# A two-layer encoder trunk on one core: pair sums by accumulating DMAs, the embedding operand split earlier, other first and last stage, and TensorE operands at other offsets modulo 256 bytes

## The chip, the cores and the metric

The kernel runs on one core of a Trainium2 chip. TensorE (PE) multiplies, its weight loads appear as PEld, VectorE (DVE), ScalarE (ACT) and GpSimd (POOL) work element by element, and DMA queues of SyncE (SP), ACT and POOL move data between HBM and SBUF. The metric is device time in microseconds (us) of one launch; less is better. One profiled execution gives the trace from which all views come.

## The reference

Two layers, one sequence of 512 tokens, width 1024, everything in 32-bit floats. Each layer does this (x holds the tokens, `g` are gains):

```python
h = rmsnorm(x, norm1_g[i])
z = h @ w_in[i] + b_in[i]                      # 12296 columns: mLSTM, retention and gates
hm = mlstm_chunkwise(...)                      # 4 heads, causal conv + silu on q and k
hr = retention_chunkwise(...)                  # 4 heads, rotary on q and k
merged = sigmoid(gm) * (y_m @ w_bm[i]) + sigmoid(gr) * (y_r @ w_br[i])
x = x + merged @ w_out[i]
h2 = rmsnorm(x, norm2_g[i])
x = x + square(relu(h2 @ w_ff1[i] + b_ff1[i])) @ w_ff2[i] + b_ff2[i]   # 4096 hidden columns
h3 = rmsnorm(x, norm3_g[i])
x = x + sigmoid(h3 @ w_pe_gate[i]) * (p[i] @ w_pe[i])                  # p: 512 x 256, the embedding
```

After the second layer `rmsnorm(x, final_g)` is the output. `rmsnorm(x, g)` is `x * rsqrt(mean(x*x) + 1e-6) * g`.

## The kernel before

**Layout.** x lies transposed in SBUF: eight tiles (`KT`) of 128 columns of the width by 512 tokens (`T`). Each fp32 operand is split in two: a high part that TensorE's fp32r type holds (a copy by ACT), and the rest, the low part (a subtraction by DVE). A product is then three matmuls, high by high, high by low, low by high (`mm3`, L295 to L298). `split` (L230 to L232) makes both parts.

**Weights.** All weights come in one stream of units of 128 x 1024 floats (512 KB), in the order of use (`wstream`, on SP's queue). `fill_raws` keeps up to four raw units (`wr`) under way; `prep_next` (L253) splits the next one into pieces `wh` and `wl`; `unit` and `ready` do so two units ahead of the matmuls that use them. A unit of kind T8 gives one tile of 128 output columns: eight steps of `mm3` with 512 moving columns, 24 matmuls, into one PSUM bank.

**Norms.** `Norm` multiplies by the gain and splits (`operand`, L388), squares (`square`, L393), adds the squares of seven tiles with POOL into `sum` (L409) and keeps the eighth as `tail`. `finish` (L411) sends sum and tail through TensorE against `ones` to get one column of token sums, and POOL takes the power -1/2 (L422). `spread` (L424) makes a row of factors from it by a diagonal matrix and TensorE (`rb`). The factor is applied to the result of a product, not to its operand, so that matmuls start before the norm is known. In the last group of ff2 each x tile that is complete goes through `Norm.tile` for norm 3 (`l0n3`, `l1n3`).

**ff1 and ff2.** `ff_order` sets the sequence: the hidden layer is made in four blocks b of four parts p. `ff1(b, p)` is two T8 units; the result is squared, cut in quarters of 256 tokens and columns, and combined to 7 operands of 256 columns (`pair_quarters`, `pair_operand`). `ff2(b, p)` is a pair of weight units with a seven-product scheme in the manner of Strassen (P1 to P7, 12 matmuls of 256 columns each, 84 in a pair). Its weight pieces are B11 (512 columns) and the sums t1, t2, t3: `prep_next` computes the sums from the two raw units r1 and r2 with four DVE additions of 128 x 512 (L269, L270, L273, L277; c0 and c1 are the two halves), then splits them. Products of P4 run one pair late (`pair_schedule`). `done` (L952) adds each product to x on DVE (L950). The tile t is a single buffer, as each of the pieces of the pair.

**Embedding.** After the last ff1 the embedding operand `pth`, `ptl` is loaded and split (L987 to L991), and two units give p @ w_pe (48 matmuls, `l0pe`, `l1pe`). Then the last group of four pairs runs, and then the gate product (`pg`).

**First stage.** Two weight units are sent for, then x in four transfers of 512 KB. The eight operands of norm 1 follow, then the other raw units, then the squares, five of them on POOL. The first unit is the small one for the input and forget gates (`l0if`); the first wide one is `l0m0z`.

**Last stage.** The last four gate units of layer 1 are kept (`LAST`), and each is run over the first 256 tokens and then over the last 256 (tiles `pl`), with one final norm for each half (`l1n40`, `l1n41`). `final` (L1047) multiplies the x tiles by the factors, three on POOL and five on DVE, and four transfers write each half.

A scheduler places the instructions in each engine's queue by the order of the program and the buffers, so that the order in a queue is not that of the text. Every engine takes its own queue in order. `shift` (L205) puts a small unused tile at the start and the end of some pools, by which the addresses of the tiles after it move.

## Time and profile before

| what | before |
|---|---|
| median of 3 runs | 2441.95 us (2439.2 to 2444.41) |
| the profiled execution | 2438.42 us |
| its span, first to last instruction | 2436.7 us |
| mean granted TensorE clock | 0.993 |
| PE busy | 2390.5 us (98%) |
| DVE, ACT, POOL busy | 1574.1, 1042.2, 142.1 us |
| moved by DMA | 241.41 MB, mean 99 GB/s |

A row of a group reads: line of the kernel, engine, operation, output<-inputs, count, shortest, median and longest duration in ns, first and last start in us, shape. A matmul's duration includes its way through the array; the time from one start to the next is shorter. A row of waits says which line of which engine waited, on whom, for how long in all, how often, and the longest. The clock is the share of full speed that the throttle granted to TensorE.

### The profile page before, as it was taken

The numbers are of one execution on the slowest core, as the hardware profiler recorded it, in microseconds if no ns is written. First come the engines' busy times: TensorE is split into PE (matmuls) and PEld (weight loads), VectorE is DVE, ScalarE is ACT, GpSimd is POOL, SyncE is SP. The second block draws the span as 40 slices with busy tenths as digits, with TensorE's granted clock in tenths as the row PEclk, the third lists the DMA queues.
The fourth block names the chain that finished last, engine by engine and source line by source line (L and its number), as shares of the span: only waits on it lengthen the run. The fifth ranks groups of instructions, "written<-read, shape, count | busy, mean of one in ns | idle before, by whom it ended". The sixth has DMA issues, their size and how long they took to land.

```text
span 2436.7 us, 30731 instructions
## 1 busy us (share of the span) xinstructions
PE 2390.5 (98%) x12220; PEld 2040.2 (84%) x12220; DVE 1574.1 (65%) x2403; ACT 1042.2 (43%) x1420; POOL 142.1 (6%) x213
## 2 busy tenths in 40 slices
PE   8999999999999999998999999999999999999997
PEld 6888888888888899898888888888888888998786
DVE  7867536663555678777778665466635547788675
ACT  4746323332333545544446552233333335445443
POOL 4100000000001000000201000000000010000012
PEclk9999999999999999999999999999999999999998
DMA  4222232223234332332322222222232342332221
GB/s 165 93 89 77 83 104 87 86 85 132 78 121 130 113 104 87 104 113 72 132 90 89 91 83 95 95 95 82 92 120 87 122 134 90 113 104 96 95 87 44
DMA packets 74417, 241.41 MB, mean 99 GB/s; under 512 B 8089, under 2 KB 10521, under 8 KB 74273
## 3 DMA queue, kind: packets, MB, share of 16 engines
q1 hardware_dynamic: 64336, 221.49, 27.3%
q10 hardware_dynamic: 9936, 17.96, 2.4%
q8 instruction: 96, 1.57, 0.3%
q14 instruction: 49, 0.39, 0.0%
HBM read 231.02 MB, written 8.39 MB: 98 GB/s over the span
## 4 chain that ended last, share of the span: by engine, by line
PE 95%; DVE 3%; ACT 1%; issue 1%; POOL 0%; DVEq 0%; ACTq 0%; POOLq 0%
PE l0f L296 2%; PE l1f L296 2%; PE l1f L297 2%; PE l0f L297 2%; PE l0f L298 2%; PE l1f L298 2%; PE l1br L297 1%; PE l1br L296 1%; PE l0br L298 1%; PE l0br L297 1%; PE l0br L296 1%; PE l1br L298 1%; PE l1bgm L296 1%; PE l0bgm L296 1%; PE l0wo L297 1%
## 5 line engine op out<-in xcount | busy, mean ns | idle before, releaser
L231 ACT ACTIVATE wh<-wr 128x1024 fp32r<-128x1024 f32 x342 | 361.7, 1059 | 851.8 <-issue 161.4
L232 DVE TENSOR_TENSOR wl<-wr,wh 128x1024 fp32r<-128x1024 f32 x342 | 419.1, 1227 | 216.0 <-ACT wh L231 215.7
L231 ACT ACTIVATE wh_t<-wr 128x1024 fp32r<-128x1024 f32 x64 | 66.9, 1058 | 84.6 <-DVE wr L270 53.6
L296 PE MATMUL l0f<-l0n2h,wh 128*128 128x512 f32 x256 | 99.8, 390 | 0.0
L296 PE MATMUL l1f<-l1n2h,wh 128*128 128x512 f32 x256 | 99.8, 390 | 0.0
L298 PE MATMUL l1f<-l1n2h,wl 128*128 128x512 f32 x256 | 99.7, 389 | 0.0
L298 PE MATMUL l0f<-l0n2h,wl 128*128 128x512 f32 x256 | 99.7, 389 | 0.0
L297 PE MATMUL l1f<-l1n2l,wh 128*128 128x512 f32 x256 | 99.7, 389 | 0.0
L297 PE MATMUL l0f<-l0n2l,wh 128*128 128x512 f32 x256 | 99.6, 389 | 0.0
L232 DVE TENSOR_TENSOR wl_t<-wr,wh_t 128x1024 fp32r<-128x1024 f32 x64 | 77.1, 1218 | 19.4 <-ACT wh_t L231 19.2
L231 ACT ACTIVATE wh_t<-t 128x1024 fp32r<-128x1024 f32 x32 | 33.9, 1061 | 58.6 <-DVE t L277 14.2
L298 PEld LDWEIGHTS l0f<-l0n2h,wl 128*128 128x128 f32 x256 | 48.1, 188 | 10.2
L298 PEld LDWEIGHTS l1f<-l1n2h,wl 128*128 128x128 f32 x256 | 48.1, 188 | 10.1
L297 PEld LDWEIGHTS l0f<-l0n2l,wh 128*128 128x128 f32 x256 | 48.1, 188 | 9.8
L297 PEld LDWEIGHTS l1f<-l1n2l,wh 128*128 128x128 f32 x256 | 48.1, 188 | 9.7
L296 PEld LDWEIGHTS l1f<-l1n2h,wh 128*128 128x128 f32 x256 | 48.1, 188 | 9.7
L296 PEld LDWEIGHTS l0f<-l0n2h,wh 128*128 128x128 f32 x256 | 48.1, 188 | 9.6
L232 DVE TENSOR_TENSOR wl_t<-t,wh_t 128x1024 fp32r<-128x1024 f32 x32 | 39.1, 1222 | 7.6 <-ACT wh_t L231 7.6
L231 ACT ACTIVATE wh_B<-wr 128x512 fp32r<-128x512 f32 x32 | 20.0, 626 | 24.6 <-issue 8.8
L409 POOL TENSOR_TENSOR l0n3sum<-l0n3sum,l0n3sq 128x512 f32<-128x512 f32 x6 | 9.4, 1572 | 348.9 <-issue 319.3
L409 POOL TENSOR_TENSOR l1n3sum<-l1n3sum,l1n3sq 128x512 f32<-128x512 f32 x6 | 8.9, 1487 | 349.3 <-ACT l1n3sum L403 319.7
L297 PE MATMUL l0pg<-l0n3l,wh 128*128 128x512 f32 x64 | 25.0, 393 | 0.2 <-DVE l0n3l L391 0.2
(3117 smaller groups left out, 7581.7 us busy)
## 6 DMA issues: line engine op xcount, KB each, us to landing
wr<-wstream SPq DMA_DIRECT2D x406, 512.0 KB, 3.3
x<-xT SPq DMA_DIRECT2D x4, 512.0 KB, 7.2
br_spill<-l0brs ACTq DMA_DIRECT2D x8, 256.0 KB, 2.0
l0brl<-br_spill ACTq DMA_DIRECT2D x8, 256.0 KB, 2.7
l0xr<-xT ACTq DMA_DIRECT2D x8, 256.0 KB, 2.7
x_spill<-l0x ACTq DMA_DIRECT2D x8, 256.0 KB, 2.2
br_spill<-l1brs ACTq DMA_DIRECT2D x8, 256.0 KB, 2.0
l1brl<-br_spill ACTq DMA_DIRECT2D x8, 256.0 KB, 2.7
```

The lines of the kernel that those rows point to most:

```text
L231: ac.activation(hi_ap, src, AF.Copy)
L232: ve.tensor_sub(lo_ap, src, hi_ap.bitcast(F32))
L296: te.matmul(o, sh, mh, start=first, stop=False)
L297: te.matmul(o, sh, ml, start=False, stop=False)
L298: te.matmul(o, sl, mh, start=False, stop=last)
L409: gp.tensor_tensor(self.sum, self.sum, sq, OP.add)
```

## The change

It has seven parts.

1. First stage: 20 matmuls of `ones` by `ones` are put at the start; one weight unit is sent for ahead of x instead of two; x comes in eight transfers of 256 KB instead of four of 512 KB; the first unit is split ahead of the operands of norm 1; the squares of norm 1 follow the first unit's product and are all on ACT.
2. Norm sums: a full-width norm adds its last square to the sum on DVE, and `finish` sends one matmul per token tile instead of two. The norms of half width stay as they were.
3. Embedding: load and split of `pth` and `ptl` stand ahead of `ff1(3, 1)`.
4. Pair sums: r1's half c0 gets r2's half c0 by an accumulating DMA on POOL's queue, right after SP's load; t's half c0 is a copy and an accumulating DMA on POOL's queue, issued with the piece B11. The two DVE additions go; the additions for t2 and for t's other half stay. The scratch for descriptors grows from 64 to 2048.
5. Norm 3 in the last group: the tiles of a pair are taken after P6 and P7 of the next pair; only the last two tiles follow the last P4.
6. Last stage: ACT multiplies each x tile by the final gain, and DVE alone multiplies by the factors, over 4 tiles at a time (4 and 4 in the first half, 4, 2 and 2 in the second), each followed by its output transfer.
7. Offsets: weights move from 224 to 0 modulo 256 bytes (`PAD`, 16 to 40 floats), and the table `OFF` sets each pool's start; its two numbers are for layer 0 and layer 1.

On DVE, in the last group of layer 0 around the end of its second pair (`l0o31`) and the start of the third (`l0o32`), these rows stand before; `l0n3l` is a low part of norm 3, `wl_t` and `wl_B` are low halves of weight pieces, `l0x` is x:

```order
L950 TENSOR_TENSOR l0x<-l0x,l0o31a 128x256
L232 TENSOR_TENSOR wl_t_9451<-t_9362,wh_t_9450 128x1024
L391 SCALAR_TENSOR_TENSOR l0n3l_9075<-l0x,bc,l0n3h_9074 128x512
L391 SCALAR_TENSOR_TENSOR l0n3l_9077<-l0x,bc,l0n3h_9076 128x512
L950 TENSOR_TENSOR l0x<-l0x,l0o32b 128x256
L269 TENSOR_TENSOR t_9491<-wr_9354,wr_9356 128x512
L950 TENSOR_TENSOR l0x<-l0x,l0o32a 128x256
L270 TENSOR_TENSOR wr_9354<-wr_9354,wr_9356 128x512
L950 TENSOR_TENSOR l0x<-l0x,l0o32c 128x256
L273 TENSOR_TENSOR wr_9356<-wr_9354,wr_9356 128x512
L277 TENSOR_TENSOR t_9491<-wr_9356,wr_9354 128x512
```

and after:

```order
L980 TENSOR_TENSOR l0x<-l0x,l0o31a 128x256
L236 TENSOR_TENSOR wl_t_9488<-t_9396,wh_t_9487 128x1024
L980 TENSOR_TENSOR l0x<-l0x,l0o32c 128x256
L401 SCALAR_TENSOR_TENSOR l0n3l_9130<-l0x,bc,l0n3h_9129 128x512
L980 TENSOR_TENSOR l0x<-l0x,l0o32b 128x256
L401 SCALAR_TENSOR_TENSOR l0n3l_9132<-l0x,bc,l0n3h_9131 128x512
L287 TENSOR_TENSOR t_9524<-wr_9394,wr_9391 128x512
L980 TENSOR_TENSOR l0x<-l0x,l0o32a 128x256
L236 TENSOR_TENSOR wl_t_9568<-wr_9394,wh_t_9567 128x1024
L980 TENSOR_TENSOR l0x<-l0x,l0o32c 128x256
L236 TENSOR_TENSOR wl_0_9654<-wr_9520,wh_0_9653 128x1024
```

The two low parts stand between the additions of the third pair's products instead of ahead of them, and two of the four sums (L269, L270) are gone.

On ACT, at the last ff1 tile of layer 0 (`l0f33st` is its staging tile, `l0hh` the high part of the hidden tile, `l0pe` the embedding product), these stand before:

```order
L923 ACTIVATE l0f33st<-l0f33st,bc 128x512
L924 ACTIVATE l0f33st<-l0f33st 128x512
L231 ACTIVATE l0hh_8988<-l0f33st 128x768
L231 ACTIVATE l0pth<-l0ptr_9089 128x512
L231 ACTIVATE l0pth<-l0ptr_9093 128x512
L231 ACTIVATE l0hh_8988<-l0f33st 128x1024
L999 ACTIVATE l0pe<-l0pe_9103 128x512
L999 ACTIVATE l0pe<-l0pe_9111 128x512
```

On ACT the two splits of the embedding now stand here, ahead of the tile `l0f31st`:

```order
L235 ACTIVATE wh_0_8817<-wr_8690 128x1024
L235 ACTIVATE wh_0_8849<-wr_8807 128x1024
L235 ACTIVATE l0pth<-l0ptr_8881 128x512
L235 ACTIVATE l0pth<-l0ptr_8885 128x512
L235 ACTIVATE wh_0_8922<-wr_8809 128x1024
L950 ACTIVATE l0f31st<-l0f31st,bc 128x512
L951 ACTIVATE l0f31st<-l0f31st 128x512
```

They moved up past six T8 units of ff1; at the old place only the hidden tile and the evacuations of the embedding product are left.

On POOL, from the last sums of norm 2 in layer 0 to norm 3, these stand before:

```order
L409 TENSOR_TENSOR l0n2sum<-l0n2sum,l0n2sq_6274 128x512
L409 TENSOR_TENSOR l0n2sum<-l0n2sum,l0n2sq_6313 128x512
L422 TENSOR_TENSOR l0n2rc<-l0n2ms,nhalf 128x4
L409 TENSOR_TENSOR l0n3sum<-l0n3sum,l0n3sq_9318 128x512
L409 TENSOR_TENSOR l0n3sum<-l0n3sum,l0n3sq_9442 128x512
```

and after, from the same place on (`t` is the summed tile, `wr` a raw unit):

```order
L421 TENSOR_TENSOR l0n2sum<-l0n2sum,l0n2sq_6305 128x512
L421 TENSOR_TENSOR l0n2sum<-l0n2sum,l0n2sq_6344 128x512
L277 DMA t_6738<-wstream 128x512
L435 TENSOR_TENSOR l0n2rc<-l0n2ms,nhalf 128x4
L278 DMA t_6738<-wstream 128x512
L259 DMA wr_6612<-wstream 128x512
L259 DMA wr_6691<-wstream 128x512
L277 DMA t_6869<-wstream 128x512
L278 DMA t_6869<-wstream 128x512
L259 DMA wr_6864<-wstream 128x512
L259 DMA wr_6984<-wstream 128x512
```

Where POOL had nothing between the two norms, it now issues the transfers of 16 pairs, three each, in this order.

```diff
@@ -48,9 +48,12 @@
 LOOK = 2
+WARM = 20
 RAWS = 4
 PIECES = 3
-PAD = 16
+PAD = 40
...
+OFF = {"xa": (0, 96), "low": (128, 224), "br": (64, 160), "n2": (192, 64), "ff": (64, 192), "n3": (32, 192)}
 LAST = 4
@@ -202,10 +205,11 @@
-    def shift(pl, side, start):
...
-        if (side == "left") == start:
-            pl.tile([P, 16 if start else 48], F32, name="shift", tag="shift")
+    def shift(pl, off, start):
...
+        w = (off if start else 256 - off) // 4
+        if w:
+            pl.tile([P, w], F32, name="shift", tag="shift" if start else "tfihs")
@@ -240,14 +244,19 @@
             loads.append((n, 0))
+    first_block = {n: b for b, (n, k) in reversed(list(enumerate(loads)))}
     place = {x: k for k, x in enumerate(order)}
...
         while at["load"] < len(loads) and sum(k[1] != "t" for k in raws) < most:
-            raws[loads[at["load"]]] = r = wpool.tile([P, UN], F32, name=f"wr{at['load']}", tag="wr", bufs=RAWS)
+            n, k = loads[at["load"]]
+            raws[n, k] = r = wpool.tile([P, UN], F32, name=f"wr{at['load']}", tag="wr", bufs=RAWS)
             nc.sync.dma_start(r, ins["wstream"][at["load"]])
+            if units[n][0] == "PAIR" and k == 0:
...
+                gp.dma_start(r[:, 0:Q], ins["wstream"][at["load"] + 1][:, 0:Q], accum_op=OP.add)
             at["load"] += 1
@@ -263,11 +272,12 @@
             if x == "B11":
+                raws[n, "t"] = t = cur["xw"].tile([P, UN], F32, name=f"t{n}", tag="t")
+                b = first_block[n]
+                gp.dma_start(t[:, c0], ins["wstream"][b][:, c0])
+                gp.dma_start(t[:, c0], ins["wstream"][b + 1][:, c1], accum_op=OP.add)
                 src, out_ = r2[:, c0], piece(cur["xw"], "b", Q)
             elif x == "t1":
-                raws[n, "t"] = t = cur["xw"].tile([P, UN], F32, name=f"t{n}", tag="t")
-                ve.tensor_tensor(t[:, c0], r1[:, c0], r2[:, c1], OP.add)
-                ve.tensor_tensor(r1[:, c0], r1[:, c0], r2[:, c0], OP.add)
                 src, out_ = r1, piece(wpool, "w")
@@ -394,7 +404,7 @@
             if self.sum is None:
-                sq = opool.tile([P, T], F32, name=f"{self.name}sum", tag="ssum" + self.half)[:, :w]
+                sq = opool.tile([P, w if self.half else T], F32, name=f"{self.name}sum", tag="ssum" + self.half)[:, :w]
             else:
@@ -403,8 +413,10 @@
                 self.sum = sq
+            elif k == KT - 1 and self.n < NT:
+                self.tail = sq
             elif k == KT - 1:
-                self.tail = sq
+                ve.tensor_tensor(self.sum, self.sum, sq, OP.add)
             else:
@@ -413,8 +425,9 @@
                 s = slice(j * P, (j + 1) * P)
-                te.matmul(o[:, 2 * j:2 * j + 2], self.sum[:, s], ones[:, 0:2], start=True, stop=False)
-                te.matmul(o[:, 2 * j:2 * j + 2], self.tail[:, s], ones[:, 0:2], start=False, stop=True)
+                te.matmul(o[:, 2 * j:2 * j + 2], self.sum[:, s], ones[:, 0:2], start=True, stop=self.n == NT)
+                if self.n < NT:
+                    te.matmul(o[:, 2 * j:2 * j + 2], self.tail[:, s], ones[:, 0:2], start=False, stop=True)
             ms = cols.tile([P, NT], F32, name=f"{n}ms", tag="ms")[:, 0:self.n]
@@ -433,7 +446,7 @@
             te.matmul(o[:, :w], ones_r, dl, start=False, stop=True)
-            self.b = opool.tile([P, T], F32, name=f"{n}rb", tag="rb" + self.half)[:, :w]
+            self.b = opool.tile([P, w if self.half else T], F32, name=f"{n}rb", tag="rb" + self.half)[:, :w]
             ac.activation(self.b, o[:, :w], AF.Copy)
@@ -605,18 +618,23 @@
     x = bpool.tile([P, KT, T], F32, name="x0", tag="big")
+    edge = phase("edge", "right")
+    edge.tile([P, 56], F32, name="edge", tag="edge")
     xa_pool = phase("xa0", "right")
+    shift(xa_pool, OFF["xa"][0], True)
     cur["low"] = phase("low0", "left")
+    shift(cur["low"], OFF["low"][0], True)
     cur["tmp"], cur["ntmp"] = cur["low"], 7
     n1 = Norm("l0n1", 0, "g1", acts(xa_pool, "l0n1"))
-    fill_raws(2)
-    for k in range(0, KT, 2):
-        nc.sync.dma_start(x[:, k:k + 2, :], ins["xT"][k:k + 2].rearrange("k p t -> p k t"))
+    warm = ps("warm")
+    for _ in range(WARM):
+        te.matmul(warm[:, 0:P], ones, ones, start=True, stop=True)
+    fill_raws(1)
+    for k in range(KT):
+        nc.sync.dma_start(x[:, k, :], ins["xT"][k])
+    ready(0)
     for k in range(KT):
         n1.operand(k, x[:, k, :])
-    fill_raws()
-    for k in range(KT):
-        n1.square(k, x[:, k, :], k < 5)
     nc.sync.dma_start(ident, ins["ident"])
@@ -654,6 +674,9 @@
             mm3(og, wh[:, s], wl[:, s], xa[0][k], xa[1][k], k == 0, k == KT - 1)
+        if i == 0:
+            for k in range(KT):
+                n1.square(k, x[:, k, :])
@@ -936,6 +963,9 @@
+        def tile3(c):
+            n3.tile(c, x[:, c, :])
@@ -960,9 +990,11 @@
                         add(0, o, OP.add)
-                        if b == 3:
-                            for c in (2 * p, 2 * p + 1):
-                                n3.tile(c, x[:, c, :])
+                        if b == 3 and p == 3:
+                            tile3(6)
+                            tile3(7)
+                    if b == 3 and p and x_ in ("P6", "P7"):
+                        tile3(2 * p - 2 + (x_ == "P7"))
@@ -977,18 +1009,21 @@
                 group = []
+            if (b, p) == (3, 1):
+                pth, ptl = [cur["ff"].tile([P, 2, T], F32R, name=f"l{i}pt{a}", tag=f"h{a}", bufs=5) for a in "hl"]
+                for k in range(2):
+                    t = tmp(f"l{i}ptr{k}")
+                    nc.scalar.dma_start(t, ins["pT"][i, k])
+                    split(t, pth[:, k, :], ptl[:, k, :])
             ff1(b, p)
+        shift(n2_pool, OFF["n2"][i], False)
         n2_pool.release()
         n3_pool = phase(f"n3{i}", act_side)
+        shift(n3_pool, OFF["n3"][i], True)
         n3 = Norm(f"l{i}n3", i, "g3", acts(n3_pool, f"l{i}n3"))
         pe = n3_pool.tile([P, KT, T], F32, name=f"l{i}pe", tag="pe")
-        pth, ptl = [cur["ff"].tile([P, 2, T], F32R, name=f"l{i}pt{a}", tag=f"h{a}", bufs=5) for a in "hl"]
-        for k in range(2):
-            t = tmp(f"l{i}ptr{k}")
-            nc.scalar.dma_start(t[:, :T], ins["pT"][i, k])
-            split(t[:, :T], pth[:, k, :], ptl[:, k, :])
         for u in range(2):
@@ -1042,18 +1078,15 @@
             cur["tmp"].release()
+            shift(n3_pool, OFF["n3"][i], False)
             n3_pool.release()
-    def final(n):
-        for c in range(KT):
-            if c < 3:
-                gp.tensor_tensor(x[:, c, n.s], x[:, c, n.s], n.b, OP.mult)
-            else:
-                ve.scalar_tensor_tensor(x[:, c, n.s], x[:, c, n.s], n.col(c), n.b, OP.mult, OP.mult)
-        for c0, c1 in ((3, 6), (0, 2), (6, 8), (2, 3)):
-            nc.sync.dma_start(out[c0:c1, :, n.s].rearrange("c p t -> p c t"), x[:, c0:c1, n.s])
...
-    for c in range(3):
+    def final(n, c0, c1):
+        v = x[:, c0:c1, n.s]
+        ve.tensor_tensor(v, v, n.b.rearrange("p (a t) -> p a t", a=1).to_broadcast([P, c1 - c0, n.n * P]), OP.mult)
+        nc.sync.dma_start(out[c0:c1, :, n.s].rearrange("c p t -> p c t"), v)
...
+    for c in range(KT - LAST):
         ac.activation(x[:, c, :], x[:, c, :], AF.Copy, scale=nn[0].col(c))
@@ -1067,17 +1100,22 @@
             pe_evac(o, c, n.s, [n])
+            ac.activation(x[:, c, n.s], x[:, c, n.s], AF.Copy, scale=n.col(c))
             if a == 1 and c == KT - LAST:
                 nn[0].finish()
-            if a == 1 and c == KT - LAST + 1:
-                nn[0].spread()
-                final(nn[0])
+            elif a == 1 and c < KT - 1:
+                if c == KT - LAST + 1:
+                    nn[0].spread()
+                final(nn[0], 4 * (c - KT + LAST - 1), 4 * (c - KT + LAST))
     nn[1].finish()
     nn[1].spread()
-    final(nn[1])
+    for c0, c1 in ((0, 4), (4, 6), (6, 8)):
+        final(nn[1], c0, c1)
     cur["tmp"].release()
     cur["last"].release()
+    shift(n3_pool, OFF["n3"][L - 1], False)
     n3_pool.release()
+    edge.release()
     assert at["unit"] == NU and at["prep"] == len(order) and not pieces and not raws and at["load"] == len(loads)
@@ -1176,7 +1214,7 @@
     }
-    nc = bacc.Bacc("TRN2", target_bir_lowering=False, num_devices=1, dynamic_dma_scratch_size=64)
+    nc = bacc.Bacc("TRN2", target_bir_lowering=False, num_devices=1, dynamic_dma_scratch_size=2048)
     aps = {n: nc.dram_tensor(n, v.shape, mybir.dt.from_np(v.dtype), kind="ExternalInput").ap()
...
     out = nc.dram_tensor("out", (KT, P, T), F32, kind="ExternalOutput").ap()
```

11 lines of the change are left out of this document (9 added, 2 removed).

## The prediction

> **What bounds the kernel now.** I read the page's first and fourth parts first, then PE's waits, then a table of stretches, and last the groups of single tiles.
>
> ```profile
> span 2436.7 us, 30731 instructions
> PE 2390.5 (98%) x12220; PEld 2040.2 (84%) x12220; DVE 1574.1 (65%) x2403; ACT 1042.2 (43%) x1420; POOL 142.1 (6%) x213
> PE 95%; DVE 3%; ACT 1%; issue 1%; POOL 0%; DVEq 0%; ACTq 0%; POOLq 0%
> ```
>
> PE is busy for 98% of the span and holds 95% of the chain that ended last. Time can leave in two ways only: PE's few waits (46 us in all), or the length of a matmul. The waits (line that waits, what it waits for, total, times, longest):
>
> ```profile
> PE l0if L296 <- ACT l0n1h L390: 8.4, 1, 8.4
> PE l0pe L296 <- ACT l0pth L231: 4.2, 1, 4.2
> PE l1pe L296 <- ACT l1pth L231: 4.2, 1, 4.2
> PE l0o33a L338 <- DVE l0x L950: 2.0, 1, 2.0
> PE l1o32a L338 <- DVE l1x L950: 1.9, 1, 1.9
> ```
>
> And the stretches: length, then busy time of PE, PEld, DVE, ACT and POOL, the granted clock, the share of the DMA engines, GB/s.
>
> ```profile
> 8.43:18.64 10.21, 9.44 (x26) 6.45 (x27) 10.21 (x10) 6.95 (x12) 10.21 (x9) 1.00 0.66 244
> 840.00:1100.00 260.00, 259.95 (x1628) 234.92 (x1627) 202.99 (x301) 127.62 (x153) 0.00 (x0) 1.00 0.30 101
> 1101.40:1119.30 17.90, 13.74 (x49) 10.71 (x49) 9.96 (x13) 10.93 (x16) 0.00 (x0) 0.81 0.17 59
> 1119.30:1175.00 55.70, 50.54 (x380) 47.40 (x379) 43.41 (x62) 23.89 (x32) 9.76 (x7) 0.97 0.25 86
> 2320.20:2375.50 55.30, 49.37 (x381) 46.28 (x380) 43.42 (x62) 24.98 (x34) 9.39 (x7) 1.00 0.28 86
> ```
>
> The pair groups of ff2 and their ff1 (840 to 1100 us) hold no wait: 259.95 of 260 us. The idle time sits at the start, in front of the embedding product (1101.40), in the last pair group of each layer (1119.30 and 2320.20), and at the end.
>
> **First stage.** Before, the first matmul starts at 8.43 us and the first wide unit (`l0m0z`) at 18.64, since DVE makes the eight low parts slowly while POOL squares the same tiles:
>
> ```profile
> 8.43 0.80 PE L296 MATMUL l0if<-l0n1h,wh 128*128 128x512 f32 x1 [8.43 <-ACT l0n1h L390]
> 18.64 0.40 PE L297 MATMUL l0m0z<-l0n1l,wh 128*128 128x512 f32 x1
> L391 DVE SCALAR_TENSOR_TENSOR l0n1l<-x,bc,l0n1h x8: 737/1523/1773, 8.5 to 16.5; 128x512 fp32r<-128x512 f32 x8
> L391 DVE SCALAR_TENSOR_TENSOR l0n2l<-l0x,bc,l0n2h x8: 742/746/747, 769.4 to 807.5; 128x512 fp32r<-128x512 f32 x8
> L391 DVE SCALAR_TENSOR_TENSOR l0n3l<-l0x,bc,l0n3h x8: 745/1550/1835, 1133.0 to 1171.4; 128x512 fp32r<-128x512 f32 x8
> L231 ACT ACTIVATE wh<-wr x342: 1040/1062/1067, 4.9 to 2382.4; 128x1024 fp32r<-128x1024 f32 x171
> L232 DVE TENSOR_TENSOR wl<-wr,wh x342: 1201/1224/2309, 6.0 to 2383.7; 128x1024 fp32r<-128x1024 f32 x171
> ```
>
> The changed code puts unit 0 first in the queue as before, so its split by DVE runs from 6.0 to 7.2 us; then eight low parts follow at 0.746 us (no POOL square beside them, as in `l0n2l`), to 13.2; then unit 1's low half, to 14.4. The data keep up: bc, unit 0 and all of x are 2.6 MB, 2.3 MB had come by 8.43 us before, and at 244 GB/s the rest is there by 9.8. Unit 1's low half is first used by its third matmul, 0.45 us into the unit, so `l0m0z` starts in effect at 13.95: 18.64 - 13.95 = 4.7 us less. The squares go to ACT, behind the first unit; only the row sums need them, a unit later. The 20 new matmuls on `ones` run on an idle PE: they cost nothing if they are over by about 8 us, when the first low part of x is there. If they hold PE until 10, the 24 matmuls of the first unit (5.4 us) end at 15.4. Bounds: -3 by that, and -6 if DVE starts on x before its weight split and the clock, at 0.80 us for a matmul still half, is full by then.
>
> **Norm sums.** Each of six full norms sends 8 records fewer (4 token tiles, two records each):
>
> ```profile
> L416 PE MATMUL l0n1ss<-ones,l0n1sum x8: 240/251/251, 29.3 to 30.8; 128*128 128x2 f32 x8
> L417 PE MATMUL l0n1ss<-ones,l0n1sq x8: 251/251/251, 29.5 to 31.0; 128*128 128x2 f32 x8
> ```
>
> Sixteen records start between 29.3 and 31.0 us, 0.113 us apart, so 8 x 0.113 x 6 = -5.4 us. The last square is now added on DVE (0.69 us, as any 128x512 sum there) behind POOL's chain of sums; the norm is finished after a unit of 24 matmuls (5.4 us), which covers it. If that cover is gone, 0.69 us in each of six, +4.1: the bounds are -5.4 and -1.3. What queues behind this addition on DVE are the next weight splits, which are two units ahead.
>
> **Embedding.** Its data are sent for at 819 us, 286 us ahead, but their split is queued behind the last ff1 tile on ACT and DVE:
>
> ```profile
> L990 ACTq DMA_DIRECT2D l0ptr<-pT x2: 334/395/456, 818.7 to 819.0; - x2
> L231 ACT ACTIVATE l0pth<-l0ptr x2: 612/612/613, 1105.1 to 1105.6; 128x512 fp32r<-128x512 f32 x2
> 1108.55 1.23 DVE L232 TENSOR_TENSOR l0hl<-l0f33st,l0hh 128x1024 fp32r<-128x1024 f32 x1
> L296 PE MATMUL l0br<-l0yr0h,wh x64: 389/389/390, 551.6 to 594.4; 128*128 128x512 f32 x64
> L298 PE MATMUL l0br<-l0yr0h,wl x64: 389/389/390, 552.0 to 594.8; 128*128 128x512 f32 x64
> ```
>
> In `l0br` 192 matmuls start in the 43.2 us from 551.6 to 594.8, 0.226 us apart. The embedding is 48 matmuls, 10.9 us, and took 17.9: a wait of 4.2, and 2.8 us at a clock of 0.81 that follows the wait. With the operands ready both go: 2 x 7.0 = -14.0. The two ACT (0.61 us) and two DVE (0.68 us) splits per layer lie beside the fully busy PE of 840 to 1100 us. Next late is the last hidden tile: complete at 1109.78, 8.4 us after 1101.40, so 2.5 us before PE comes to it, and earlier now with the embedding's four splits out of its way. Bounds: -14, and -11 if that tile takes those 2.5 us and 0.5 more in one layer and the clock dips.
>
> **Last pair group.** In each layer PE idles 55.70 - 50.54 = 5.2 and 55.30 - 49.37 = 5.9 us, since DVE, between two pairs, has two additions of a weight sum and two low parts (`l0n3l`, 1.55 us beside POOL's sums) ahead of the addition into x that frees a bank. After, the low parts follow P6 and P7 of the next pair, and the two sums are no longer DVE's. DVE's work in the stretch falls from 43.4 us by 4 x 2 x 0.68 to 38.0, against 50 of PE. Per pair that is about 8.4 us of splits and additions and two low parts of 0.75 to 1.55: 9.9 to 11.5, against 9.9 us of PE (84 matmuls). So some wait may stay where POOL's sums stretch a low part. Bounds -11.1 and -5; I take three quarters, -8.5.
>
> **Last stage.** DVE's five products of each half run as one stretch:
>
> ```profile
> 2419.67 3.56 DVE L1052 SCALAR_TENSOR_TENSOR l1x<-l1x,bc,l1n40rb 128x256 f32<-128x256 f32 x5 [0.45 <-ACT l1n40rb L437]
> 2429.08 3.57 DVE L1052 SCALAR_TENSOR_TENSOR l1x<-l1x,bc,l1n41rb 128x256 f32<-128x256 f32 x5 [1.09 <-ACT l1n41rb L437]
> ```
>
> The first lies in front of the last tile's gate, the second in front of the last output transfer: both on the path. They become products over four tiles (1024 columns, 1.22 us, as the weight split) or two (0.68): 2 x 1.22 = 2.44, and 1.22 + 2 x 0.68 = 2.58, DVE alone and without POOL beside it. -1.1 and -1.0, together -2.1; the added ACT scalings follow each square. Bounds -3 (a first output that leaves earlier) and +1 (the scaling of the last tile holds up ACT's copy of `l1n41rb`).
>
> **Sums by DMA.** 64 DVE sums of 0.68 us go, and 96 DMAs of 256 KB on POOL's queue come, 64 of them accumulating, which no row shows.
>
> ```profile
> L269 DVE TENSOR_TENSOR t<-wr,wr x32: 677/684/1427, 842.4 to 2349.7; 128x512 f32<-128x512 f32 x32
> L270 DVE TENSOR_TENSOR wr<-wr,wr x32: 677/683/694, 845.4 to 2351.4; 128x512 f32<-128x512 f32 x32
> br_spill<-l0brs ACTq DMA_DIRECT2D x8, 256.0 KB, 2.0
> l0brl<-br_spill ACTq DMA_DIRECT2D x8, 256.0 KB, 2.7
> wr<-wstream SPq DMA_DIRECT2D x406, 512.0 KB, 3.3
> ```
>
> There the DVE gain is worth nothing (PE never waits from 840 to 1100), outside the last group counted above. The tile `t` has one buffer: POOL's copy waits for the split of the pair before (1.06 + 1.22 = 2.3 us), its accumulation waits for the copy, the next accumulation for SP's load. Copy and accumulation must fit in 9.9 - 2.3 = 7.6 us of a pair; by the nearest rows they take 2.0 to 3.3 each. POOL's queue also carries the norm's sums behind these waits, with over a pair to spare. The 25 MB more are a tenth of 241, at a DMA share of 0.30 in this stretch. I take +1 (a late first sum in a few groups); bounds 0 and the slow case below.
>
> **Residues.** The weights move to offset 0 modulo 256 bytes and the moving operands to another multiple of 32 bytes in each stage; before, nearly all stood at 224. Counted from the built programs' addresses, 108 matmuls of 512 columns have stationary and moving operand at unequal residues before and 6036 after; of those of 256 columns 2692 have before (hidden tiles at 32) and 2884 after.
>
> ```profile
> L297 PE MATMUL l0pe<-l0ptl,wh x16: 388/392/760, 1107.2 to 1118.9; 128*128 128x512 f32 x16
> L298 PE MATMUL l0pe<-l0pth,wl x16: 393/394/629, 1107.7 to 1119.1; 128*128 128x512 f32 x16
> L338 PE MATMUL l0o00a<-l0hh,wh_t x12: 280/280/382, 866.2 to 873.2; 128*128 128x256 f32 x12
> L297 PE MATMUL pl<-l1n3l,wh x64: 279/283/284, 2391.9 to 2418.3; 128*128 128x256 f32 x64
> ```
>
> Unequal residues stand beside 392 to 394 ns against 389 at 512 columns (`l0pe`), but beside 280 against 283 at 256 (`l0o00a` unequal, `pl` equal). The matmuls concerned have 512 columns, but `l0pe` is the one disturbed stretch of the program, so neither row is near enough to decide. The bounds are (392 - 389) x 6036 = +18 us and -3 x 6036 = -18; I take -1 ns each, -6 us, since the undisturbed rows are those that gain.
>
> The rows also show a part that does not grow with the columns: 256 columns more cost 389 - 283 = 106 ns, so 512 would be 212, and a matmul starts every 226, which leaves 14 ns. Whether placement can free it is the third rival.
>
> The Trainium skill ("TensorE: Matmul & The Clock Gate", section "Wait — 56ns, not 53.3ns?") gives 215.7 ns from start to start at 512 columns on a warm clock, with a fixed cost of about 2.5 ns; the trace's 226 ns differs. By the page 6036 x 10.5 ns would be 63 us off, and the sum 2345.
>
> **Sum.** -4.7 - 5.4 - 14.0 - 8.5 - 2.1 + 1 - 6 = -39.7: a span of 2397.0. The profiled execution took 2438.42, 1.7 more than its span, and the median of the three runs is 3.5 above that: 2397.0 + 1.7 + 3.5 = 2402.
>
> **Rivals.** *Residues hurt*: the case of `l0pe` holds everywhere, +18 in place of -6, and 2426. Speaks for it: it is the only 512-column row; against: its disturbed clock. 2417 to 2437, chance 0.12.
>
> *The sums by DMA are slow, slower than before*: the place is the loop through `t`. With a copy of 2.0 us it holds PE once an accumulation takes longer than 5.6 us; each further us costs 32, one per pair, and at 6.9 us (1.3 x 32 = 41) the whole gain is gone; at 8 us the time would be 2478. For it: no row shows an accumulating DMA, and POOL issues all three in order; against: 2.0 to 3.3 us for the same bytes, and the load's queue at 0.30. Chance 0.17, of it 0.03 about as before, 0.14 slower. The Trainium skill ("SBUF — State Buffer", box on the "DVE blocks DMA" trap) says that transfers issued by GpSimd wait for their descriptors while DVE runs in a two-port mode; no run here shows it.
>
> *The residues free the matmul*: `l0o00a` against `pl` is the sign that a residue acts. Were the 14 ns gone from 6036 matmuls, -84 in place of -6, the time would be 2324; against it, at 256 columns an unequal residue frees 3 ns of the 14. Partial relief lies between 2324 and 2385. Chance 0.12, of it 0.05 below 2375.
>
> *The stalls only move*: the hidden tile, or a low part, takes the place of the waits that go; then only norms, first and last stage count (-12.2 and +1), 2431 without a gain by residues. Chance 0.03, as good as excluded for the embedding by the 2.5 us to spare.
>
> **Numbers.** The forecast has 0.56. A measurement of this kernel tells about 0.2% (4.9 us) from no change. Faster 0.80, same 0.06 (0.03 slow sums, the rest the upper ends of the other cases), slower 0.14. The forecast's own range is 2385 to 2417; the range for 8 in 10 reaches from 2375, part of the freed matmul, to 2442, the residues that hurt and the first of the slow sums.
>
> **What would show it.** Right: `l0pe` and `l1pe` no longer among PE's waits, and 10.9 us long; the last pair groups with under 2 us of idle time in each; 8 records in `l0n2ss`; `l0m0z` at about 14 us; matmuls of 387 to 389 ns. Wrong: a row in which PE waits on a low part of a `t` piece or on ACT's `wh_t` from `t` once per pair (slow sums); 512-column durations that differ by stage by more than 3 ns (residues: the table differs in each stage, so this is read directly); a clock below 0.99 in a new place.

## The result: slower by 2.3%

The changed kernel takes 2497.26 us (median of 4 runs, 2492.89 to 2501.03) against 2441.91 before: a ratio of 1.0226, 95% interval 1.0202 to 1.0250. The forecast was 2402, in a range to 2442. The profiled execution took 2494.08 us with a span of 2492.4.

The first lines of the page of the changed kernel (span, busy time, the chain that ended last by engine and by line, two rows of DMA issues):

```profile
span 2492.4 us, 30966 instructions
PE 2427.4 (97%) x12212; PEld 2045.8 (82%) x12212; DVE 1535.8 (62%) x2340; ACT 1047.8 (42%) x1434; POOL 196.6 (8%) x298
PE 86%; DMA 7%; DVE 3%; issue 2%; ACT 1%; POOL 0%; POOLq 0%; DVEq 0%; ACTq 0%; SPq 0%
t<-wstream POOLq DMA_DIRECT2D x64, 256.0 KB, 4.3
wr<-wstream POOLq DMA_DIRECT2D x32, 256.0 KB, 4.0
```

Two things happened at once. PE is busy 37 us longer (2427.4 against 2390.5) with about as many records (12212 against 12220), so its matmuls got longer; the granted clock, 0.991 against 0.993, makes an estimated 5 us of it (0.002 x 2492). And PE's idle time grew from 46 to 65 us although the waits that the change was to remove are gone; DMA, which had no share of the chain, now has 7%.

PE's waits after (five of their rows, in the form that the prediction shows):

```profile
PE l0o32a L348 <- DVE l0x L980: 2.7, 1, 2.7
PE l1o23c L348 <- DVE l1x L980: 2.5, 1, 2.5
PE l0o03c L348 <- DVE l0x L978: 2.4, 1, 2.4
PE l0o23c L348 <- DVE l0x L980: 1.9, 1, 1.9
PE l0o13c L348 <- DVE l0x L980: 1.6, 1, 1.6
```

and the stretch that held no wait before:

```profile
840.00:1100.00 260.00, 241.14 (x1518) 214.85 (x1517) 173.76 (x256) 113.46 (x137) 26.48 (x35) 0.99 0.45 127
```

The wait on `l0pth` is no longer a row, nor is the 8.4 us wait of the first stage. In their place nearly every pair (`o03`, `o13`, `o23`, the pairs of the last group) waits for DVE's addition into x, and from 840 to 1100 us PE idles 18.9 us where it idled 0.05.

The chain of waits between 979 and 992 us names what DVE waits for (start, length, what):

```profile
979.19 1.06 ACT wh_t L235
980.27 1.23 DVE wl_t L236
981.50 0.34 DVE l0x L980
981.86 3.89 DMA t<-wstream
985.75 0.35 issue
986.10 5.83 DMA t<-wstream
992.04 1.07 ACT wh_t L235
```

This is one turn of the loop through the single tile t: split by ACT and DVE, POOL's copy, POOL's accumulation, the next split. From one `wh_t` to the next it takes 992.04 - 979.19 = 12.85 us, and a pair has 9.9 us of matmuls. DVE meets the low part `wl_t` in its queue, and the additions that free the PSUM banks stand behind it. The pages show this wait for all 32 pairs (count, busy us and mean ns, then idle time in front and what ended most of it): before, DVE stood 7.6 us in front of the low part of t, after, 51.3, and ACT in front of the high part waits for the DMA:

```profile
L232 DVE TENSOR_TENSOR wl_t<-t,wh_t 128x1024 fp32r<-128x1024 f32 x32 | 39.1, 1222 | 7.6 <-ACT wh_t L231 7.6
L236 DVE TENSOR_TENSOR wl_t<-t,wh_t 128x1024 fp32r<-128x1024 f32 x32 | 39.1, 1223 | 51.3 <-ACT wh_t L235 51.2
L235 ACT ACTIVATE wh_t<-t 128x1024 fp32r<-128x1024 f32 x32 | 33.8, 1057 | 109.8 <-DMA t<-wstream 89.2
```

The longer matmuls show in the groups of single tiles. All have 512 columns; the difference of the moving operand's and the weights' residue modulo 256, by the built program's addresses, is 0 in `l0bgm`, 64 in `l0br`, 128 in `l0wo`, 192 in `l0f`, 96 in `l1bgm`, 224 in `l1wo`, 160 in `l1br`:

```profile
L308 PE MATMUL l0bgm<-l0n1h,wl x64: 388/389/397, 61.1 to 259.5; 128*128 128x512 f32 x64
L306 PE MATMUL l0br<-l0yr0h,wh x64: 394/394/397, 547.3 to 590.6; 128*128 128x512 f32 x64
L307 PE MATMUL l0br<-l0yr0l,wh x64: 388/388/397, 547.5 to 590.8; 128*128 128x512 f32 x64
L308 PE MATMUL l0br<-l0yr0h,wl x64: 392/392/394, 547.8 to 591.0; 128*128 128x512 f32 x64
L306 PE MATMUL l0wo<-l0mh,wh x64: 390/393/404, 758.9 to 802.8; 128*128 128x512 f32 x64
L308 PE MATMUL l0f<-l0n2h,wl x256: 393/394/398, 804.0 to 1125.4; 128*128 128x512 f32 x128
L308 PE MATMUL l1bgm<-l1n1h,wl x64: 392/394/399, 1287.1 to 1490.3; 128*128 128x512 f32 x64
L306 PE MATMUL l1wo<-l1mh,wh x64: 393/396/397, 2001.4 to 2045.5; 128*128 128x512 f32 x64
L306 PE MATMUL l1br<-l1yr0h,wh x64: 392/397/400, 1785.1 to 1829.4; 128*128 128x512 f32 x64
```

All these groups had a median of 389 ns before. Of these stages only the one at equal residues kept it for all three products.

### The profile page after: what moved, and what is told of

It reads as the page before. It is cut to its first block, busy times and chain, and to the rows that moved or that the text cites. A ratio compares the mean times of both kernels' runs of the same rounds, so it can differ in the third digit from the quotient of the medians.

```text
span 2492.4 us, 30966 instructions
## 1 busy us (share of the span) xinstructions
PE 2427.4 (97%) x12212; PEld 2045.8 (82%) x12212; DVE 1535.8 (62%) x2340; ACT 1047.8 (42%) x1434; POOL 196.6 (8%) x298
## 4 chain that ended last, share of the span: by engine, by line
PE 86%; DMA 7%; DVE 3%; issue 2%; ACT 1%; POOL 0%; POOLq 0%; DVEq 0%; ACTq 0%; SPq 0%
DMA t<-wstream 6%; PE l0f L306 2%; PE l0f L307 2%; PE l1f L306 2%; PE l0f L308 2%; PE l1f L308 2%; PE l1f L307 2%; PE l1br L308 1%; PE l1br L306 1%; PE l1br L307 1%; PE l0br L306 1%; PE l0br L308 1%; PE l0br L307 1%; ACT wh_t L235 1%; DMA wr<-wstream 1%
## 5 line engine op out<-in xcount | busy, mean ns | idle before, releaser
L236 DVE TENSOR_TENSOR wl_t<-t,wh_t 128x1024 fp32r<-128x1024 f32 x32 | 39.1, 1223 | 51.3 <-ACT wh_t L235 51.2
L259 POOL DMA_DIRECT2D wr<-wstream x32 | 27.3, 852 | 390.7 <-DMA wr<-wstream 170.0
L278 POOL DMA_DIRECT2D t<-wstream x32 | 27.5, 858 | 101.8 <-DMA t<-wstream 101.8
L277 POOL DMA_DIRECT2D t<-wstream x32 | 20.1, 628 | 118.5 <-DVE wl_t L236 83.6
```

The lines of the kernel that those rows point to most:

```text
L236: ve.tensor_sub(lo_ap, src, hi_ap.bitcast(F32))
L259: gp.dma_start(r[:, 0:Q], ins["wstream"][at["load"] + 1][:, 0:Q], accum_op=OP.add)
L277: gp.dma_start(t[:, c0], ins["wstream"][b][:, c0])
L278: gp.dma_start(t[:, c0], ins["wstream"][b + 1][:, c1], accum_op=OP.add)
```

## The experiments

**Both causes taken apart.** Theory: the residues and the sums by DMA each cost time, they add, and the rest of the change saves what was forecast. Rivals: one of the two causes carries it all, or the removed stalls only moved.

The changed kernel with the old residues (weights and nearly all moving operands at 224 modulo 256 again; the descriptor scratch moves the base of SBUF, hence 32 for `PAD`):

```diff
-PAD = 40
+PAD = 32
-OFF = {"xa": (0, 96), "low": (128, 224), "br": (64, 160), "n2": (192, 64), "ff": (64, 192), "n3": (32, 192)}
+OFF = {'xa': (0, 0), 'low': (0, 0), 'br': (0, 0), 'n2': (0, 0), 'ff': (64, 64), 'n3': (0, 0)}
...
-    edge.tile([P, 56], F32, name="edge", tag="edge")
+    edge.tile([P, 64], F32, name="edge", tag="edge")
```

> The changed kernel with every operand back at the residues of before (224 nearly everywhere). Theory (two causes that add): in the changed trace the 512-column matmuls start 233 ns apart at most unequal residues against 227 at equal ones, about 30 us over the program, so the time falls from 2497 to about 2467, and the waits in the pair groups (54 us of them) stay. Rival (the sums by DMA alone): 2497, no change beyond 5 us. Rival (residues alone): about 2405.

Measured 2463.14 us (2461.26 to 2464.20), 1.0084 of before (1.0069 to 1.0099): 34 us less than the changed kernel.

The changed kernel with the two sums on DVE and its new residues:

```diff
-            if units[n][0] == "PAIR" and k == 0:
-                gp.dma_start(r[:, 0:Q], ins["wstream"][at["load"] + 1][:, 0:Q], accum_op=OP.add)
...
-                gp.dma_start(t[:, c0], ins["wstream"][b][:, c0])
-                gp.dma_start(t[:, c0], ins["wstream"][b + 1][:, c1], accum_op=OP.add)
...
+                raws[n, "t"] = t = cur["xw"].tile([P, UN], F32, name=f"t{n}", tag="t")
+                ve.tensor_tensor(t[:, c0], r1[:, c0], r2[:, c1], OP.add)
+                ve.tensor_tensor(r1[:, c0], r1[:, c0], r2[:, c0], OP.add)
```

> The changed kernel with the two sums of a pair back on DVE and no DMA on POOL's queue, the new residues kept. Theory (two causes that add): the waits in the first three pair groups of each layer (39 us in the changed trace) go and the last groups keep a few us, so 2497 falls by 40 to 50, to 2447-2457. Rival (residues alone): 2497 within 10 us. Rival (the sums alone): about 2407.

Measured 2437.23 us (2436.14 to 2439.71), 0.9981 (0.9971 to 0.9990): 60 us less than the changed kernel, 10 more than forecast. The forecast counted the waits of the first three groups of a layer and took those of the last groups as staying; but there too PE's waits on additions fell (`l0o32a` from 2.7 to 1.7 us, `l0o33a` from 2.9 to 1.1). It also left out the clock: between the two profiled executions PE's idle time fell by 39.5 us (65.0 to 25.5), and its busy time by 14.9 (2427.4 to 2412.5) at the same residues, with a granted clock of 0.996 against 0.991.

Both edits together:

> The changed kernel with the old residues and the sums on DVE, so that the first and last stage, the norm sums, the embedding and the low parts in the last group are what is left of the change. Prediction on record for these terms: -4.7 - 5.4 - 14.0 - 8.5 - 2.1 = -34.7, so 2407 (2400 to 2415). Rival (the stalls move on): 2431. By subtraction from the changed kernel (2497 - 30 - 45) it would be 2422.

Measured 2406.49 us (2405.45 to 2407.71), 0.9853 (0.9837 to 0.9870). That is 34.8 us under the kernel before in the same set of runs (2441.3), against 34.7 forecast for these terms. It is faster than both kernels. With it the four corners of the square are there: sums by DMA cost 2463.1 - 2406.5 = 56.7 us at old residues and 2497.3 - 2437.2 = 60.0 at new ones; the new residues cost 30.7 us with sums on DVE and 34.1 with sums by DMA. The causes add within 4 us.

Of what the sums by DMA cost, only a part is waiting. At old residues the two profiled executions differ by 56.2 us of span (2461.0 and 2404.8): PE's idle time makes 40.4 of it (64.0 against 23.6), and its busy time 15.8 (2397.0 against 2381.2), although the residues are the same. The granted clock is 0.992 against 0.997. That alone makes an estimated 12 us (0.008 x 2461 - 0.003 x 2405), so most of the longer busy time is lost clock: the trace has eight stretches of 3.4 us at half clock that the other lacks.

The residues alone, on the kernel before (the table `OFF` and the `shift` lines of the change, `PAD` 24 for the same addresses):

> The kernel of before with the offsets of the changed kernel and nothing else. Theory (two causes that add): +30 us by the start-to-start times of the changed trace, 2472. Prediction on record: -6 (bounds -18 and +18), 2436. Rival (the sums alone): 2442.

Measured 2469.95 us (2467.68 to 2472.47), 1.0113 (1.0098 to 1.0128): +28.7 us.

**Which DMA.** Theory: the loop through t. Rival: r1's accumulation, which delays a raw unit, or any transfer of POOL's queue. All three start from the run with both causes back. They were measured in a later set, in which the kernel before took 2443.4 us instead of 2441.3; the differences below are between medians, and by the ratios to before they are 47, 3 and 10 us.

```diff
+                gp.dma_start(t[:, c0], ins["wstream"][b][:, c0])
+                gp.dma_start(t[:, c0], ins["wstream"][b + 1][:, c1], accum_op=OP.add)
...
-                ve.tensor_tensor(t[:, c0], r1[:, c0], r2[:, c1], OP.add)
                 ve.tensor_tensor(r1[:, c0], r1[:, c0], r2[:, c0], OP.add)
```

> Old residues and all other parts of the change; of the two sums, t's is made by copy and accumulating DMA, r1's by DVE. Theory (the loop through the single tile t: split 2.3 us, copy about 4.2 and accumulation about 5.9 with their issues, 12.4 to 12.9 us against 9.9 of PE per pair): nearly all of the 57 us stay, 2455 to 2463. Rival (r1's accumulation, which holds the raw unit back by 4 us, is what costs): 2407 to 2415.

Measured 2455.32 us (2452.08 to 2457.54): +48.8 of the 56.7, at the lower end of the theory's range.

```diff
+                gp.dma_start(r[:, 0:Q], ins["wstream"][at["load"] + 1][:, 0:Q], accum_op=OP.add)
...
                 ve.tensor_tensor(t[:, c0], r1[:, c0], r2[:, c1], OP.add)
-                ve.tensor_tensor(r1[:, c0], r1[:, c0], r2[:, c0], OP.add)
```

> Old residues and all other parts of the change; r1's sum by the accumulating DMA, t's on DVE. The sum for t takes r1 with r2's half already in it, so its values are not those of the reference; amounts and order of the work are. Theory (the loop through t): 2405 to 2412, since four raw units are under way and 4 us more fit in two pairs. Rival (r1's accumulation): 2455 to 2463.

Measured 2410.99 us (2409.13 to 2413.11): +4.5.

```diff
+                gp.dma_start(t[:, c0], ins["wstream"][b][:, c0])
...
-                ve.tensor_tensor(t[:, c0], r1[:, c0], r2[:, c1], OP.add)
+                ve.tensor_tensor(t[:, c0], t[:, c0], r2[:, c1], OP.add)
                 ve.tensor_tensor(r1[:, c0], r1[:, c0], r2[:, c0], OP.add)
```

> As the run with t alone by DMA, but only the copy is left to POOL's queue and DVE adds the second term. Theory (the length of the loop): split 2.3, copy 4.2 and DVE's addition 0.7 make 7.2 us, under the 9.9 of a pair, so 2405 to 2412. Rival (any transfer of POOL's queue behind the split in front of t holds PE, by descriptors that are late while DVE works or by the queue itself): above 2425.

Measured 2417.05 us (2415.30 to 2420.71): +10.6, between the two forecasts and nearer the theory's. With the loop under a pair's time 38 us of the 49 are gone, so its length is the main cost. What stays does not look like the loop: in the first three groups of each layer the second and third turn take 9.8 to 10.1 us from one `wh_t` to the next, a pair's time. DVE's addition now stands in an ordered queue behind the copy:

```profile
L278 DVE TENSOR_TENSOR t<-t,wr x32: 676/692/696, 836.0 to 2335.3; 128x512 f32<-128x512 f32 x32
...
its engine sat idle before it (us, times) until:
  DMA t<-wstream: 10.2, 18
```

DVE sat idle 10.2 us in front of it in 18 of 32 pairs, which is about the size of the 10.6; that the one is the other was not tried by itself. A second buffer for t, which would open the loop without a change to its transfers, was not tried either.

**The rule of the residues.** From the traces I took the time between back-to-back starts, and from the built programs the operands' addresses (mean ns of groups of at least 179 matmuls; a range where runs or stages differ):

| difference modulo 256 | 512 columns | 256 columns |
|---|---|---|
| 0 | 226.9 to 227.2 | 119.3 to 119.5 |
| 32, 96, 224 | 233.1 to 233.4 | |
| 64 | 229.0 to 229.9 | 116.2 to 117.5 |
| 128 | 232.4 | 118.6 |
| 160 | 234.1 to 234.2 | |
| 192 | 233.3 | 115.2 to 115.8 |

Two runs test that the difference decides and not the residue: the kernel before with weights, and the pools on their side, 64 bytes lower and 64 bytes higher, by `PAD` alone (16 to 0, 16 to 32).

> The kernel of before with the weights and the pools on their side 64 bytes lower: 4140 of the 512-column matmuls stay equal at 160, 3534 get moving 224 against weights 160 (difference 64), 576 get 160 against 224 (difference 192). Theory (the difference decides; 229.1 ns at 64, 233.3 at 192, 227 at 0): 3534 x 2.2 + 576 x 6.4 = 11.5 us, and a little for 768 matmuls of 256 columns that come to a difference of 128, so 2453 (2450 to 2457). Rival (any unequal pair costs alike, 6.4 ns): 2467. Rival (absolute residues): no forecast from the rows, 2442.

> The kernel of before with the weights and the pools on their side 64 bytes higher: 4184 of the 512-column matmuls stay equal at 32, 3480 get moving 224 against weights 32 (difference 192), 576 get 32 against 224 (difference 64), 768 of 256 columns become equal. Theory (the difference decides): 3480 x 6.4 + 576 x 2.2 + 768 x 1.8 = 25 us, so 2466 (2462 to 2470). Rival (any unequal pair costs alike): 2467, so that the two runs together tell them apart. Rival (absolute residues): 2442.

Measured 2459.26 us (2455.68 to 2460.19), 1.0068 (1.0053 to 1.0083), and 2467.55 us (2463.08 to 2472.19), 1.0105 (1.0083 to 1.0128). The second is as forecast. The first is 6 above and outside its range; 229.9 ns where 229.1 was put in (3459 x 0.8 = 2.8 us) and 118.6 at the 256-column difference of 128 (757 x 1.1 = 0.8 us) explain 3.6 of the 6. So the difference decides in the main, but does not fix the time to the nanosecond: in this run the stages at 64 start between 229.0 and 230.7 ns apart. That every unequal pair costs alike would have given 2467 in both: the first run's interval excludes it. Absolute residues are out: 512 columns at 160 by 160 and at 32 by 32 both start 227.2 ns apart.

The 256-column matmuls like 192, so the run with both causes back was made with hidden tiles at 160:

```diff
-OFF = {..., 'ff': (64, 64), ...}
+OFF = {..., 'ff': (192, 192), ...}
```

> The changed kernel with old residues and sums on DVE, and the hidden tiles at 160 instead of 32 (weights at 224, so the difference goes from 64 to 192 modulo 256). Theory (a matmul's spacing goes by the difference of the residues and by the columns): the 256-column matmuls fall from 117.5 to about 115.5 ns as in the changed kernel's layer 1, 2688 x 2 ns = 5 us, so about 2401; l0pe and l1pe lose 0.4 us. Rival (the spacing depends on the absolute residues, or pairs are held by DVE): 2406.5 within 2 us.

Measured 2406.05 us (2404.63 to 2407.25), 0.9846 (0.9833 to 0.9860): not told apart from 2406.49. The spacing fell as foreseen, from 117.5 to 115.2 ns, but the groups of four pairs only from 41.2 to 40.9 us on average, and PE's busy time fell by 3.1 us (2381.2 to 2378.1) while its idle time grew by 2.2 (23.6 to 25.8; the wait `l0o32a` on DVE's addition went from 1.7 to 1.9). So 0.9 us of span are left of the 5 expected, and the runs do not resolve them. That DVE's additions pace the pairs here is a reading of these waits and was not tried by itself.

**Two terms alone, on the kernel before.** The embedding:

```diff
+            if (b, p) == (3, 1):
+                pth, ptl = [cur["ff"].tile([P, 2, T], F32R, name=f"l{i}pt{a}", tag=f"h{a}", bufs=5) for a in "hl"]
+                for k in range(2):
+                    t = tmp(f"l{i}ptr{k}")
+                    nc.scalar.dma_start(t[:, :T], ins["pT"][i, k])
+                    split(t[:, :T], pth[:, k, :], ptl[:, k, :])
             ff1(b, p)
...
-        pth, ptl = [cur["ff"].tile([P, 2, T], F32R, name=f"l{i}pt{a}", tag=f"h{a}", bufs=5) for a in "hl"]
...
```

> The kernel of before with load and split of the embedding operand ahead of ff1(3, 1) and nothing else. Theory (the wait of 4.2 us and the clock dip behind it both go): -14, about 2427. Rival (the wait goes, the dip comes back in the last pair group or the hidden tile is late): -8 to -10, 2432.

Measured 2428.60 us (2425.92 to 2430.88), 0.9947 (0.9927 to 0.9967): -13.2. The stretch of the embedding product in this run:

```profile
1101.20:1112.00 10.80, 10.80 (x49) 8.86 (x48) 8.79 (x11) 9.48 (x14) 0.00 (x0) 1.00 0.29 98
```

It has no idle time and full clock, against 17.9 us at 0.81 before. A part of the rival holds too: behind it, from 1112 to 1165 us, the last pair group has a granted clock of 0.94, where it had 0.97 (1119.30:1175.00) before, so some of the dip moved there.

The low parts of norm 3 in the last group:

```diff
-                        if b == 3:
-                            for c in (2 * p, 2 * p + 1):
-                                n3.tile(c, x[:, c, :])
+                        if b == 3 and p == 3:
+                            n3.tile(6, x[:, 6, :])
+                            n3.tile(7, x[:, 7, :])
+                    if b == 3 and p and x_ in ("P6", "P7"):
+                        c = 2 * p - 2 + (x_ == "P7")
+                        n3.tile(c, x[:, c, :])
```

> The kernel of before with the low parts of norm 3 spread over P6 and P7 of the next pair and nothing else. Prediction on record for this term together with two DVE sums less in each pair: -8.5 (-11.1 to -5). The trace of the run with both causes back shows -3.1 and -2.9 us for the last group and the gate's start in the two layers, the sums being on DVE there: theory -6, 2436. Rival (the waits move to the end of the group): within 2 us of 2441.

Measured 2432.56 us (2431.85 to 2433.03), 0.9962 (0.9947 to 0.9976): -9.3 by the medians, -5.9 by the spans of the two profiled executions (2436.7 and 2430.8). The waits did not move to the end of the group.

## Why the prediction was wrong

**Sums by DMA: the step that failed first.** "Copy and accumulation must fit in 9.9 - 2.3 = 7.6 us of a pair; by the nearest rows they take 2.0 to 3.3 each." The bound was right, the durations were not, the accumulation's above all. In the chain shown, the copy has landed at 985.75, 4.2 us after the split's end at 981.50, and the accumulation at 991.93, 6.2 us after that, both with their issues: together 10.4 us, 2.8 over. The medians over all 32 pairs hide this: from the start of the issue to the landing they are 3.2 us for the copy, inside the range, and 4.8 for the accumulation, together 8.0. But in the first turn of a group there is time to spare (about 25 us from split to split). In the second and third the two took 8.9 to 10.7 us together, 10.0 on average. In six of the eight second turns the copy was the slow one (5.4 to 6.7 us), in the third turns the accumulation (5.8 to 7.3). With t alone by DMA, so without r1's transfers in the same queue, the second turn's copies took 2.9 to 3.2, and its accumulations still 4.8 to 7.1; why these are slow there was not settled. The nearest rows were plain transfers of ACT's and SP's queues; these are POOL's, whose issue alone occupies POOL for 0.57 us (copy) and 0.85 us (accumulation), and whose accumulation lands later:

```profile
L278 POOL DMA_DIRECT2D t<-wstream x32: 846/852/917, 811.4 to 2408.1; - x32
...
DMA to landing us min/median/max: 3.7/4.8/7.3
```

The rival named the place and the price per microsecond. Its 32 per microsecond over-counts: the first pair of a group has its t made ahead (`l0o00a` to `l0o02a` takes 18.5 us with and without the DMAs), which leaves three turns in each of eight groups. At old residues these are 2.2, 3.5 and 2.6 us longer on average than with DVE's sums, 67 us in all, and the step to the next group gives 12 back; 57 to 60 were measured. Group by group it is 5 to 9 us, the lost clock with it. The prediction's own signs of slow sums came in another form: PE's rows name DVE's additions, not the pieces of t, since the wait on `wh_t` is DVE's and PE meets only what stands behind it; and a clock under 0.99 in a new place is there, 0.94 from 1153.5 to 1180 us. I gave this rival 0.17. The rows could have said more: the slack was 7.6 us for two transfers in a chain that no row priced, and an upper end of 3.3 was the longest of a kind that was not this one.

**Residues: the term that was mis-sized.** -6, between -18 and +18; measured +28.7 alone. Two errors. `l0pe` was set aside as disturbed, but its 388, 392 and 394 ns are those that `l0br` shows after, undisturbed, at the same difference of 64. And 64 is the cheapest of the unequal differences: of 6036 matmuls some 1630 are there, the others stand at 32, 96, 128, 160, 192 and 224, which cost 5.5 to 7.2 ns each against the 1 ns gained that the sum put in and the 3 ns of its bound. With the table: 1630 x 2.2 + 4400 x 6.6 = 33 us, less 3 us for the 256-column matmuls, makes 30. No row shown of before has any difference but 0 and 64, and the bound was taken from one of them.

The third rival, that residues free the matmul, is out for 512 columns: no difference came below the 226.9 ns of equal residues. The Trainium skill ("TensorE: Matmul & The Clock Gate", section "Wait — 56ns, not 53.3ns?") gives 215.7 ns there; no group of a run here reached it.

**What was right.** From the run with both causes back, beside the profile before:

```profile
1106.90:1157.00 50.10, 46.48 (x362) 43.94 (x361) 42.67 (x62) 24.29 (x33) 9.12 (x6) 1.00 0.28 95
```

```profile
13.50 0.39 PE L302 MATMUL l0m0z<-l0n1h,wh 128*128 128x512 f32 x1
14.13 0.50 PE L304 MATMUL l0m0z<-l0n1h,wl 128*128 128x512 f32 x1
```

```profile
L424 PE MATMUL l0n1ss<-ones,l0n1sum x8: 231/251/251, 24.7 to 25.5; 128*128 128x2 f32 x8
```

```profile
2389.72 2.36 DVE L1082 TENSOR_TENSOR l1x<-l1x,l1n40rb 128x1024 f32<-128x1024 f32 x2 [0.45 <-ACT l1n40rb L446]
2397.93 2.43 DVE L1082 TENSOR_TENSOR l1x<-l1x,l1n41rb 128x1024 f32<-128x1024 f32 x3 [1.09 <-ACT l1n41rb L446]
```

- First stage, -4.7: `l0m0z` starts at 13.50 and waits 0.17 for its third matmul, so 13.7 in effect against 13.95 foreseen; the norm's sums start at 24.7 against 29.3, 4.6 earlier. The last warming matmul starts at 7.61, and `l0if` follows at 7.64.
- Norm sums, -5.4: eight records in place of sixteen, which start over 0.7 to 0.8 us instead of 1.6 to 1.9, so 0.9 to 1.1 us less at each of six norms.
- Embedding, -14.0: -13.2 alone. The hidden tile was not late.
- Last pair group, -8.5: -5.9 in spans, -9.3 in medians, alone. PE still idles 50.10 - 46.48 = 3.6 us there (5.2 before), where the prediction looked for under 2. The part of it that the two missing DVE sums were to give is not separate: with the sums by DMA the group got longer, not shorter.
- Last stage, -2.1: 2.36 and 2.43 us against 2.44 and 2.58 foreseen. From the first matmul of `pl` to the end it takes 42.99 us against 44.89, 1.9 less, of which 0.7 lies behind the second half's factors.

Their sum was forecast as -34.7 and came as -34.8. That it agrees to 0.1 us is luck: the two terms that were run alone are each off by about 1 us in opposite directions, the sums were on DVE in this run though -8.5 counted two fewer, and the other three terms are read from the trace and were not run alone. The sign of the whole hung on two terms that the trace before did not show, and together they were given -5: they cost 90.8 (2497.3 - 2406.5).

## What to carry to other kernels

A transfer that replaces an addition must be priced by its chain, not by the engine it relieves: count the turn of the buffer that it closes (here split, copy, accumulation, 12.85 us) against the work per turn (9.9), and take no duration from another queue as its upper end. DVE stood idle 57 of the 260 us from 840 to 1100, so the additions were free where they stood (PE idled 0.05 us there). And a wait costs more than its length when the clock falls after it, here 15.8 us of longer matmuls, an estimated 12 of them by the clock, beside 40.4 of waiting. Where a placement changes for many instructions, ask how many distinct cases the old trace shows: here two differences of residues out of eight, one of them taken for noise, and a bound drawn from them held for neither side of the forecast.

## What the runs showed of the hardware

- A matmul's start-to-start time depends on the difference of its two operands' residues modulo 256 bytes: 226.9 ns at 0 to 234.2 at 160 with 512 columns, and the other way with 256 columns (119.3 at 0, 115.2 at 192). The weight load lasts 187 to 192 ns (medians) whatever the difference. Why the sign turns with the columns was not settled.
- At a difference of 64 the three products of a step last 388, 392 and 394 ns, mostly in a fixed order, which begins at another of the three in another stage (`l0br` with 394, `l0pe` of before with 388).
- An accumulating transfer of 256 KB on POOL's queue occupies POOL 0.85 us. Those of t land 4.8 us after the start of their issue in the median and 7.3 at most, those of r1 4.0 and 4.7. A plain copy there occupies POOL 0.57 us and lands after 3.2 us in the median and 6.7 at most. Plain 256 KB transfers of ACT's queue landed in 2.0 to 2.7.
- After waits in the pair groups of the changed kernel some matmuls of 256 columns started 213 ns apart, 9 to 16 in a row, against 115 to 120 elsewhere; the granted clock is 0.50 there, for 3.4 us each time (from 1169.3 us, for one). In the run with both causes back no pair group has such a stretch.
